# Softmax probabilities: transposes on TensorE replaced by one DMA transpose of fp16 parts per unit

## The chip, the cores and the metric

The kernel runs on one core of a Trainium2 chip. A core has five engines with instruction queues of their own, each worked through in order: TensorE (PE, whose weight loads are listed as PEld), VectorE (DVE), ScalarE (ACT), GpSimd (POOL) and SyncE (SP), whose queue issues all DMAs here. The engines meet through semaphores. The metric is the device time of one execution, in microseconds.

## The reference

Two transformer layers on 1024 tokens of width 1024, in fp32, each with two kinds of attention side by side. Layer one has A (each query keeps the 256 best keys by a cheap indexer's score) and B (a window of 128 with a learned sink); layer two has C (each query attends three times: to compressed blocks, to selected blocks, to a window of 512) and D (latent attention with a rope part). Each has 8 heads. The part that matters, from D:

```python
p = jnp.exp(s - m)
p = p / jnp.maximum(jnp.sum(p, axis=-1, keepdims=True), 1e-30)
o = jnp.einsum('bhqs,bshd->bqhd', p.astype(v.dtype), v)
```

With sequences this short nothing is dropped from C's selection. Scores are large, so products must be near fp32 accuracy.

## The kernel before

Each fp32 operand of a product is held as a high and a low part, and a product is made of three matmuls (high by high, high by low, low by high).

The work is written as Python generators. `attn_gen` yields attention work; `fill_gen` and others yield projection or output matmuls, which `Lanes.run` puts between attention steps by a ratio. A scheduling pass then fixes each engine's final order.

Attention is done by query block of 128 rows (i = 0 to 7) and by group of 4 heads. The unit of work is one pass of the loop over `h0`: as many heads as fit into 1024 columns of scores (4 heads up to 256 keys, 2 up to 512, else 1). So a block with 1, 2, 3, 4 or more times 128 keys is 1, 1, 2, 2 or 4 units. Over a group of 8 blocks A has 22 units, D has 22, B has 8; C has 52, its three branches being 8, 22 and 22. The two groups double this: 208 units. C works through its blocks in the order 0, 1, 4, 5, 6, 7, 2, 3 in group 0 and 0, 1, 2, 3, 6, 7, 4, 5 in group 1.

In a unit TensorE makes the scores (`psS`, line 636), VectorE adds the mask and takes the maximum (`pt`, `nm`, line 639), ScalarE applies Exp (line 644). In groups of up to four 128×128 blocks, `tstage` then transposes the fp32 probabilities on TensorE into PSUM (`psT`, line 664), and they are cut there into fp16 parts `ph` and `pl` in one of two ways, chosen by `WAYS`: "p" has ScalarE write `ph` (668) and VectorE `pl` (669); "q" has ScalarE copy to `sg` (673) and GpSimd make both (674, 675). `cstage` multiplies them with the values into `po` (682 to 684). A unit's transposes are issued about one unit after its scores. C's three branches are added up in `cacc` and stored by a DMA (1295). Weights come by DMA into `wraw` (442), a ring of two, are rounded by ScalarE (446), and GpSimd makes the low part (447).

Of the kernel before, what the change touches and what calls it, by code (L numbers as in the profile page):

```python
# [36 lines left out]
WW = 280  # L37
RG = 0.375
PSCALE = 4096.0
SLOT = 2048  # L40
QB = 3
TR = 1.4
# [12 lines left out]
SR = 0.6  # L55
GDA = [2, 3, 4, 7], [5, 6]
WR = 2
WBF = 14
BO = [2, 3, 0, 1, 4, 5, 6, 7], [2, 3, 0, 1, 4, 5, 6, 7]
AO = list(range(NT)), list(range(NT))  # L60
CO = [0, 1, 4, 5, 6, 7, 2, 3], [0, 1, 2, 3, 6, 7, 4, 5]
# [3 lines left out]
SQB = 1  # L65
RPB = 1
PTC = 1
PHB = 4
PTB = 3
CSB = 1  # L70
SG = 2
WAYS = ('q', 'q', 'ppq', 'pq', 'ppq', 'pq', 'ppq', 'p')
ENG = 'nz zc ky'
ENG2 = 'nz dy ky dq'
MANUAL = False
# [87 lines left out]
def trunk(ctx: ExitStack, tc: tile.TileContext, A, out):  # L163
# [11 lines left out]
    wpool = es_w.enter_context(tc.tile_pool(name="wp", bufs=1, side="right"))  # L175
    dr = ctx.enter_context(tc.tile_pool(name="dr", bufs=1, space=bass.MemoryType.DRAM))
    psA = {n: ctx.enter_context(tc.tile_pool(name=n, bufs=2, space=PSUM)) for n in ("pp", "psS")}
    psT = ctx.enter_context(tc.tile_pool(name="psT", bufs=3, space=PSUM))
    psO = ctx.enter_context(tc.tile_pool(name="psO", bufs=1, space=PSUM))
    if MANUAL:  # L180
        ctx.enter_context(tc.manual_schedule())

# [146 lines left out]
    def tps():  # L329
        return psT.tile([P, 4, P], F32, name="psT")  # L330
# [202 lines left out]
    def v_scale(m, res):  # L533

        yield from L.take_in("psT", PTC)
        ps = tps()
        T.transpose(ps[0:1, 0], m, identf)
        yield
        r = st.tile([P, 2], F32, name="vs_r")
        V.tensor_reduce(r[0:1, 0:1], ps[0:1, 0], AX.X, OP.max)  # L540
        V.tensor_scalar(r[0:1, 0:1], r[0:1, 0:1], 2.0 ** -90, None, op0=OP.max)
        yield
        T.matmul(ps[:, 1, 0:1], r[0:1, 0:1].to_broadcast([1, P]), identf[0:1, 0:1], start=True, stop=True)
        yield
# [6 lines left out]
        V.tensor_scalar(e[:, 0:1], e[:, 0:1], 2.0 ** -15 / PSCALE, None, op0=OP.mult)  # L551
        yield
        res.append((e[:, 1:2], e[:, 0:1]))

# [32 lines left out]

    def attn_gen(jobs):

        tq, cq = [], []  # L590

        def do_T():
            cq.append(tq.pop(0)()[0])

        def do_C():
            cq.pop(0)()

        for jb in jobs:
            while jb.get("drain") and (tq or cq):
                if tq:  # L600
                    do_T()
                else:
                    do_C()
                yield 300
            for ev in jb["need"]:
                yield ev
            nk, npass = jb["nk"], jb["npass"]
# [13 lines left out]
            for h0 in range(0, 4, per):  # L621
# [3 lines left out]
                for j, h in enumerate(hs):  # L625
                    first = init(h)
                    step = 320 if nk == 640 else 512
                    for c in range(0, nk, step):
# [11 lines left out]
                                               -1.0, first, op0=OP.add, op1=OP.min, accum_out=low)  # L640
                        first = low
                        at += w
                for j, h in enumerate(hs):
                    S.activation(pt[:, j * nk:(j + 1) * nk], pt[:, j * nk:(j + 1) * nk], AF.Exp, scale=-1.0,  # L644
                                 bias=nm[:, h:h + 1], accum_out=sm[:, h:h + 1])
                yield per * npass * max(107, nk * 0.42)
                if h0 + per == 4:
# [4 lines left out]
                todo = [(h, kt, j * nk + kt * P) for j, h in enumerate(hs) for kt in range(max(1, nk // P))]  # L652
                if cmp_:
                    todo = [(2 * a, 0, a * P) for a in range(2)]
                for c in range(0, len(todo), 4):
                    grp = todo[c:c + 4]
                    lastg = h0 + per == 4 and c + 4 >= len(todo)

                    def tstage(jb=jb, grp=grp, pt=pt, lastg=lastg, vh=vh, vl=vl, nk=nk, get_po=get_po, fin=fin, cmp_=cmp_,
                               fb=fbox if h0 + per == 4 else None):  # L660
                        n = len(grp)
# [3 lines left out]
                        ph = wk.tile([P, 4, P], F16, name="ph", bufs=PHB)  # L665
                        pl = wk.tile([P, 4, P], F16, name="pl", bufs=PHB)
                        if next(jb["way"]) == "p":
                            S.activation(ph[:, :n], pT[:, :n], AF.Copy, scale=PSCALE)  # L668
                            V.scalar_tensor_tensor(pl[:, :n], pT[:, :n], PSCALE, ph[:, :n], op0=OP.mult,  # L669
                                                   op1=OP.subtract)  # L670
                        else:
                            sg = wk.tile([P, 4, P], F32, name="sg", bufs=SG)
                            S.activation(sg[:, :n], pT[:, :n], AF.Copy, scale=PSCALE)  # L673
                            G.tensor_scalar(ph[:, :n], sg[:, :n], 1.0, 1.0, op0=OP.mult, op1=OP.mult)  # L674
                            G.tensor_tensor(pl[:, :n], sg[:, :n], ph[:, :n], OP.subtract)  # L675

                        def cstage():
                            po = get_po()
                            nt = max(1, nk // P)
                            for a, (h, kt, o) in enumerate(grp):  # L680
                                dst = po[:, h:h + 2].rearrange("p h d -> p (h d)") if cmp_ else po[:, h]
                                T.matmul(dst, ph[:, a], vh(kt, h), start=kt == 0, stop=False)  # L682
                                T.matmul(dst, ph[:, a], vl(kt, h), start=False, stop=False)  # L683
                                T.matmul(dst, pl[:, a], vh(kt, h), start=False, stop=kt == nt - 1)  # L684
                            if lastg:
                                assert fb
                                fin(po, fb[0])
                            return n * 87 + (0 if not lastg else 1)
                        return cstage, n * 110
                    tq.append(tstage)  # L690

                while len(tq) > jb["tlag"](len(todo)):
                    c_, cost = tq.pop(0)()
                    cq.append(c_)
                    yield cost
                    while len(cq) > 1:
                        yield cq.pop(0)()
        while tq:
            c_, cost = tq.pop(0)()
            cq.append(c_)  # L700
            yield cost
            while len(cq) > 1:
                yield cq.pop(0)()
        while cq:
            yield cq.pop(0)()

    def softmax_norm(mul=None):

# [964 lines left out]
    def out_tile(i):  # L1673
        mh = D["mh", i]
        for c in range(2):
            xr = D["pool"].tile([P, 512], F32, name="xr", bufs=XB)
# [121 lines left out]
```

## Time and profile before

| | |
|---|---|
| three runs, median (lowest, highest) | 1559.89 us (1559.67, 1560.49) |
| the profiled execution, its span | 1559.19 us, 1557.4 us |
| busy: TensorE, VectorE, ScalarE, GpSimd | 1384.3, 1226.1, 869.8, 821.4 us |
| mean granted TensorE clock | 0.946 |

The span runs from the first to the last instruction of the profiled execution. Busy time is the union of an engine's instruction times. Matmuls are pipelined and their ends are modelled, so that one instruction's duration is more than the time by which it delays the next; the distance between two starts in the timeline gives that. The parts follow each other so: projections and indexer scores up to about 150 us; the top-k search, with B's units put in between, up to 467; A's two groups up to 628; the first output projection and the second layer's projections up to 840; C, with further projections, up to 1230; D, with the last output projection, to the end.

### The profile page before, as it was taken

How to read it: one execution, taken by the hardware profiler on the slowest of the kernel's cores; microseconds unless marked ns; L12 is line 12 of the kernel's file. 1: busy time of each engine (PE TensorE's matmuls, PEld its weight loads, DVE VectorE, ACT ScalarE, POOL GpSimd, SP SyncE). 2: the span in 40 equal slices, each digit the busy share in tenths (PEclk: the TensorE clock that was granted, in tenths of full speed). 3: DMA queues.
4: the chain of work that ended last, by engine and by line, in shares of the span. 5: the costliest groups of instructions: out<-in, count | busy, mean ns of one | idle time of the engine just before them, and what ended most of it. 6: DMA issues, size and time to landing. Idle time of an engine off the chain costs nothing.

```text
span 1557.4 us, 35155 instructions
## 1 busy us (share of the span) xinstructions
PE 1384.3 (89%) x12588; PEld 1273.9 (82%) x12588; DVE 1226.1 (79%) x3827; ACT 869.8 (56%) x2385; POOL 821.4 (53%) x1097
## 2 busy tenths in 40 slices
PE   6998888788637889999999999999999778889999
PEld 6888878788636779999999998899988556778887
DVE  8599999999998876428338668976689999996763
ACT  6354576577406766325424666956667666754531
POOL 4767642467777657324447343565456565652240
PEclk9999999989867999999999999999999879989999
DMA  6311212111102132332312210012100210111232
GB/s 199 86 35 32 57 56 71 43 36 33 45 17 69 59 107 76 111 108 86 82 36 55 66 49 8 9 47 63 33 15 19 78 62 15 32 55 59 95 112 75
DMA packets 88431, 93.19 MB, mean 60 GB/s; under 512 B 20928, under 2 KB 73152, under 8 KB 88256
## 3 DMA queue, kind: packets, MB, share of 16 engines
q1 hardware_dynamic: 88256, 90.95, 19.3%
q8 instruction: 99, 1.62, 0.4%
q14 instruction: 76, 0.62, 0.1%
HBM read 67.85 MB, written 23.07 MB: 58 GB/s over the span
## 4 chain that ended last, share of the span: by engine, by line
PE 48%; DVE 33%; DMA 6%; POOL 5%; issue 5%; ACT 3%; SPq 0%; POOLq 0%; DVEq 0%; ACTq 0%
PE psS L636 8%; PE pp L490 7%; PE pp L492 6%; PE pp L491 6%; PE psT L664 6%; DVE junk L845 6%; DVE pt L639 4%; PE pp L1683 2%; PE pp L1681 2%; PE pp L1682 2%; PE po L684 2%; PE po L682 2%; PE po L683 2%; DMA wraw<-in_ab_w_in 1%; POOL wlo L447 1%
## 5 line engine op out<-in xcount | busy, mean ns | idle before, releaser
L490 PE MATMUL pp<-whi,Rh 128*128 128x256 f32 (+4 forms) x1648 | 489.1, 297 | 25.9 <-DVE zst L581 9.9
L492 PE MATMUL pp<-whi,Rl 128*128 128x256 f32 (+4 forms) x1648 | 481.0, 292 | 0.6 <-DVE Rl L327 0.6
L491 PE MATMUL pp<-wlo,Rh 128*128 128x256 f32 (+4 forms) x1648 | 480.0, 292 | 0.0
L490 PEld LDWEIGHTS pp<-whi,Rh 128*128 128x128 f32 x1648 | 322.5, 196 | 33.1 <-DVE zst L581 13.9
L644 ACT ACTIVATE pt<-pt,nm 128x256 f32<-128x256 f32 (+8 forms) x384 | 246.6, 643 | 178.6 <-DVE nm L639 173.3
L492 PEld LDWEIGHTS pp<-whi,Rl 128*128 128x128 f32 x1648 | 321.1, 195 | 2.2 <-DVE Rl L327 1.1
L491 PEld LDWEIGHTS pp<-wlo,Rh 128*128 128x128 f32 x1648 | 322.0, 196 | 1.0
L447 POOL TENSOR_TENSOR wlo<-wraw,whi 128x256 fp32r<-128x256 f32 (+4 forms) x208 | 162.3, 787 | 189.6 <-ACT whi L446 176.9
L664 PE MATMUL psT<-identf,pt 128*128 128x128 f32 x1256 | 216.1, 284 | 14.2 <-DVE pl L669 4.2
L674 POOL TENSOR_SCALAR ph<-sg 128x512 f16<-128x512 f32 (+3 forms) x157 | 89.3, 570 | 157.9 <-ACT sg L673 142.0
L664 PEld LDWEIGHTS psT<-identf,pt 128*128 128x128 f32 x1256 | 147.3, 143 | 28.1 <-issue 4.3
L675 POOL TENSOR_TENSOR pl<-sg,ph 128x512 f16<-128x512 f32 (+3 forms) x157 | 163.4, 1041 | 8.7
L446 ACT ACTIVATE whi<-wraw 128x256 fp32r<-128x256 f32 (+4 forms) x208 | 83.7, 416 | 125.0 <-DMA wraw<-in_cd_w_in 37.8
L669 DVE SCALAR_TENSOR_TENSOR pl<-psT,ph 128x512 f16<-128x512 f32 (+3 forms) x233 | 128.4, 556 | 26.8 <-ACT ph L668 26.4
L668 ACT ACTIVATE ph<-psT 128x512 f16<-128x512 f32 (+3 forms) x233 | 111.9, 492 | 51.7 <-PE psT L664 49.2
L684 PEld LDWEIGHTS <-pl 128*128 128x128 f16 x1256 | 114.2, 99 | 26.1 <-issue 7.4
L682 PEld LDWEIGHTS <-ph 128*128 128x128 f16 x1256 | 116.7, 100 | 20.0 <-issue 7.9
L683 PEld LDWEIGHTS <-ph 128*128 128x128 f16 x1256 | 116.7, 100 | 14.7 <-issue 13.5
L639 DVE CUSTOM_DVE_ANT_0 pt<-psS,mk 128x512 f32<-128x512 f32 (+4 forms) x208 | 107.1, 518 | 23.7 <-PE psS L636 21.8
L673 ACT ACTIVATE sg<-psT 128x512 f32<-128x512 f32 (+3 forms) x157 | 83.4, 534 | 32.7 <-PE psT L664 30.1
L344 POOL TENSOR_TENSOR nz<-nz,rs_y 128x512 f32<-128x512 f32 (+2 forms) x44 | 41.2, 937 | 94.0 <-DVE rs_y L288 68.2
L636 PE MATMUL psS<-ka,qs 128*128 128x512 f32 (+4 forms) x192 | 58.7, 405 | 24.1 <-DVE nm L639 23.8
(311 smaller groups left out, 3622.4 us busy)
## 6 DMA issues: line engine op xcount, KB each, us to landing
wraw<-in_cd_w_in SPq DMA_DIRECT2D x72, 128.0 KB, 2.1
wraw<-in_ab_w_in SPq DMA_DIRECT2D x56, 128.0 KB, 2.2
xs<-in_x SPq DMA_DIRECT2D x8, 512.0 KB, 6.0
od<-mx SPq DMA_DIRECT2D x32, 128.0 KB, 1.8
wraw<-in_ab_w_out SPq DMA_DIRECT2D x32, 128.0 KB, 2.2
x<-in_x SPq DMA_DIRECT2D x8, 512.0 KB, 4.6
mo<-od SPq DMA_DIRECT2D x16, 256.0 KB, 2.7
nz<-zdr SPq DMA_DIRECT2D x16, 256.0 KB, 2.8
```

The costliest lines, as they stand in the source:

```text
L447: G.tensor_tensor(lo[:, :o], raw[:, :o], hi[:, :o].bitcast(F32), OP.subtract)
L490: T.matmul(ps, xh, hi[:, :n], start=q == 0 and k == 0, stop=False)
L491: T.matmul(ps, xh, lo[:, :n], start=False, stop=False)
L492: T.matmul(ps, xl, hi[:, :n], start=False, stop=q == 3 and k == 1)
L636: T.matmul(ps[:, at + a - c:at + b - c], lhs, rhs(a, b), start=n == 0, stop=n == len(pl_) - 1)
L639: V.tensor_tensor_reduce(pt[:, j * nk + c:j * nk + c + w], ps[:, at:at + w], mask(c, w), -1.0, first, op0=OP.add, op1=OP.min, accum_out=low)
L644: S.activation(pt[:, j * nk:(j + 1) * nk], pt[:, j * nk:(j + 1) * nk], AF.Exp, scale=-1.0, bias=nm[:, h:h + 1], accum_out=sm[:, h:h + 1])
L664: T.transpose(pT[:, a], pt[:, o:o + P], identf)
L675: G.tensor_tensor(pl[:, :n], sg[:, :n], ph[:, :n], OP.subtract)
L682: T.matmul(dst, ph[:, a], vh(kt, h), start=kt == 0, stop=False)
L683: T.matmul(dst, ph[:, a], vl(kt, h), start=False, stop=False)
L684: T.matmul(dst, pl[:, a], vh(kt, h), start=False, stop=kt == nt - 1)
```

## The change

Probabilities stay in SBUF. ScalarE first adds ln 4096 to the negated maximum `nm`, so that Exp gives them already scaled. It then copies the whole unit to fp16 (`hl`, first half). VectorE or GpSimd, by `WAYS` (all units of B by GpSimd, of the others every second), writes the remainder to the second half. One DMA on SP's queue transposes all blocks of both halves into `ht`. The matmuls with the values read `ht`, one unit later (`LAG`). `hl` and `ht` have two buffers each. The remaining transposes on TensorE (of queries, keys, mixes) have two `psT` banks where there were three, `po` has two where there was one, the ring of prepared weight tiles has 13 where it had 14, and the residual tile `xr` at the end shares a ring with the last weights.

```diff
+LNP = float(np.log(PSCALE))
+HLB = 2
+HTB = 2
+LAG = 1
-WBF = 14
+WBF = 13
-WAYS = ('q', 'q', 'ppq', 'pq', 'ppq', 'pq', 'ppq', 'p')
+WAYS = ('g', 'g', 'dg', 'dg', 'dg', 'dg', 'dg', 'dg')
-    psT = ctx.enter_context(tc.tile_pool(name="psT", bufs=3, space=PSUM))
-    psO = ctx.enter_context(tc.tile_pool(name="psO", bufs=1, space=PSUM))
+    psT = ctx.enter_context(tc.tile_pool(name="psT", bufs=2, space=PSUM))
+    psO = ctx.enter_context(tc.tile_pool(name="psO", bufs=2, space=PSUM))
...
+                S.activation(nm[:, h0:h0 + per], nm[:, h0:h0 + per], AF.Copy, bias=LNP)
                 for j, h in enumerate(hs):
                     S.activation(pt[:, j * nk:(j + 1) * nk], pt[:, j * nk:(j + 1) * nk], AF.Exp, scale=-1.0,
                                  bias=nm[:, h:h + 1], accum_out=sm[:, h:h + 1])
+                n = per * nk
+                hl = wk.tile([P, 2048], F16, name="hl", bufs=HLB)[:, :2 * n]
+                S.activation(hl[:, :n], pt[:, :n], AF.Copy)
+                e = V if next(jb["way"]) == "d" else G
+                e.tensor_tensor(hl[:, n:], pt[:, :n], hl[:, :n], OP.subtract)
+                nb = n // P
+                ht = wk.tile([P, 16, P], F16, name="ht", bufs=HTB)
+                nc.sync.dma_start(ht[:, :2 * nb], hl.rearrange("p (k n) -> p k n", n=P), transpose=True)
...
-                        pT = tps()
-                        for a, (h, kt, o) in enumerate(grp):
-                            T.transpose(pT[:, a], pt[:, o:o + P], identf)
...
+                    for a, (h, kt) in enumerate(todo):
+                        dst = po[:, h:h + 2].rearrange("p h d -> p (h d)") if cmp_ else po[:, h]
+                        T.matmul(dst, ht[:, a], vh(kt, h), start=kt == 0, stop=False)
+                        T.matmul(dst, ht[:, a], vl(kt, h), start=False, stop=False)
+                        T.matmul(dst, ht[:, nb + a], vh(kt, h), start=False, stop=kt == nt - 1)
...
+                cq.append(cstage)
+                while len(cq) > LAG:
+                    yield from cq.pop(0)()
```

ScalarE's queue, in C at block 7 of group 0 (the four heads of the selected branch, 1024 columns each; `ph` and `sg` are read from PSUM), before:

```order
L644 ACTIVATE pt_14002,sm_14001<-pt_14002,nm_14000 128x1024
L644 ACTIVATE pt_13931,sm_13930<-pt_13931,nm_13929 128x64 x2
L673 ACTIVATE sg_14024<-psT_14019 128x256
L644 ACTIVATE pt_14035,sm_14001<-pt_14035,nm_14000 128x1024
L668 ACTIVATE ph_14057<-psT_14052 128x512
L668 ACTIVATE ph_14097<-psT_14092 128x512
L644 ACTIVATE pt_14121,sm_14001<-pt_14121,nm_14000 128x1024
L673 ACTIVATE sg_14145<-psT_14138 128x512
L668 ACTIVATE ph_14172<-psT_14167 128x512
L644 ACTIVATE pt_14198,sm_14001<-pt_14198,nm_14000 128x1024
```

The same place now, with the changed file's line numbers (638 is Exp, 642 the copy to `hl`, 636 the bias):

```order
L642 ACTIVATE hl_12780<-pt_12768 128x1024
L638 ACTIVATE pt_12813,sm_12767<-pt_12813,nm_12766 128x1024
L636 ACTIVATE nm_12766<-nm_12766 128x1
L642 ACTIVATE hl_12825<-pt_12813 128x1024
L638 ACTIVATE pt_12867,sm_12767<-pt_12867,nm_12766 128x1024
L636 ACTIVATE nm_12766<-nm_12766 128x1
L638 ACTIVATE pt_12925,sm_12767<-pt_12925,nm_12766 128x1024
L642 ACTIVATE hl_12879<-pt_12867 128x1024
L636 ACTIVATE nm_12976<-nm_12976 128x1
L638 ACTIVATE pt_12978,sm_12977<-pt_12978,nm_12976 128x640
L642 ACTIVATE hl_12937<-pt_12925 128x1024
```

The two reads of PSUM per unit are gone; a copy to `hl` stands between the Exps, and from the third unit of the block on it stands one Exp later than its own.

SP's queue at the same place now (1268 is the store of a finished block of C, whose last transpose is that of `ht_12674`). Before, this stretch held only such stores and weight loads:

```order
L647 DMA_TRANSPOSE ht_12592<-hl_12589 128x10x128
L647 DMA_TRANSPOSE ht_12635<-hl_12632 128x10x128
L647 DMA_TRANSPOSE ht_12674<-hl_12671 128x10x128
L647 DMA_TRANSPOSE ht_12725<-hl_12722 128x4x128
L1268 DMA od2_101<-cacc_12360 128x256
L647 DMA_TRANSPOSE ht_12783<-hl_12780 128x16x128
L647 DMA_TRANSPOSE ht_12828<-hl_12825 128x16x128
L647 DMA_TRANSPOSE ht_12882<-hl_12879 128x16x128
L647 DMA_TRANSPOSE ht_12940<-hl_12937 128x16x128
```

One transpose per unit has come in, of 4 to 16 blocks, and the store stands between the transposes of the following block.

## Rows read from the trace of the kernel before

**Rows 1.** The page: busy time, share of the span and instructions of each engine.

```profile
PE 1384.3 (89%) x12588; PEld 1273.9 (82%) x12588; DVE 1226.1 (79%) x3827; ACT 869.8 (56%) x2385; POOL 821.4 (53%) x1097
```

**Rows 2.** By stretch: start:end, length, busy PE, PEld, DVE, ACT, POOL; clock, DMA.

```profile
150.00:467.00 317.00, 240.25 (x1964) 229.26 (x1963) 310.60 (x861) 176.32 (x482) 183.23 (x219) 0.89 0.16 45
467.00:546.00 79.00, 66.45 (x677) 54.37 (x678) 67.97 (x189) 53.83 (x131) 55.27 (x65) 0.85 0.21 67
546.00:628.00 82.00, 75.11 (x871) 67.62 (x870) 55.79 (x169) 55.22 (x130) 55.13 (x67) 0.98 0.31 91
628.00:840.00 212.00, 211.27 (x1757) 208.51 (x1754) 108.35 (x319) 79.65 (x217) 85.12 (x124) 0.98 0.26 78
840.00:941.00 101.00, 100.36 (x1049) 97.75 (x1048) 69.33 (x271) 61.82 (x189) 47.33 (x67) 1.00 0.21 58
941.00:1010.00 69.00, 67.39 (x830) 58.16 (x829) 60.70 (x227) 56.66 (x162) 31.99 (x44) 1.00 0.03 10
1010.00:1134.00 124.00, 123.80 (x1265) 120.74 (x1264) 86.45 (x315) 74.89 (x227) 68.06 (x89) 1.00 0.16 46
1134.00:1230.00 96.00, 84.38 (x968) 75.79 (x967) 88.47 (x397) 65.08 (x211) 56.15 (x89) 0.98 0.10 31
1230.00:1400.00 170.00, 135.94 (x1146) 113.78 (x1147) 160.88 (x508) 112.05 (x296) 103.40 (x132) 0.86 0.14 45
1400.00:1557.00 157.00, 153.80 (x1177) 128.42 (x1175) 97.04 (x270) 61.74 (x152) 39.94 (x52) 1.00 0.26 85
```

**Rows 3.** Line 664, transposes of probabilities, by stretch: length, PE, PEld; clock, DMA.

```profile
546.00:628.00 82.00, 22.65 (x138) 15.64 (x136) 0.98 0.31 91
...
840.00:941.00 101.00, 20.17 (x111) 13.33 (x111) 1.00 0.21 58
...
1010.00:1134.00 124.00, 22.95 (x130) 15.22 (x130) 1.00 0.16 46
...
1400.00:1557.00 157.00, 20.76 (x130) 14.83 (x128) 1.00 0.26 85
```

**Rows 4.** The timeline of PE in C: start, duration, instruction.

```profile
970.50 1.09 PE L664 MATMUL psT<-identf,pt 128*128 128x128 f32 x8
971.35 1.17 PE L636 MATMUL psS<-ks,qs 128*128 128x512 f32 x4
```

**Rows 5.** Groups, partly by shape: busy us, mean ns; idle us before, releasers.

```profile
L668 ACT ACTIVATE ph<-psT 128x512 f16<-128x512 f32 (+3 forms) x233 | 111.9, 492 | 51.7 <-PE psT L664 49.2 <-PE po L683 1.0 <-PE po L684 0.8
L673 ACT ACTIVATE sg<-psT 128x512 f32<-128x512 f32 (+3 forms) x157 | 83.4, 534 | 32.7 <-PE psT L664 30.1 <-POOL pl L675 1.2 <-PE psS L636 0.4
L669 DVE SCALAR_TENSOR_TENSOR pl<-psT,ph 128x512 f16<-128x512 f32 x133 | 90.5, 682 | 12.1 <-ACT ph L668 11.7
L675 POOL TENSOR_TENSOR pl<-sg,ph 128x512 f16<-128x512 f32 x121 | 142.1, 1175 | 6.5
L510 ACT ACTIVATE pt<-x 128x1024 f32<-128x1024 f32 x8 | 8.5, 1059 | 1.7 <-DVE x L1091 1.7
L1588 ACT ACTIVATE sq<-pp 128x128 f32<-128x128 f32 x16 | 4.7, 294 | 0.0
```

**Rows 6.** Line 669, VectorE's low parts, by stretch: length, DVE; clock, DMA.

```profile
467.00:546.00 79.00, 15.03 (x27) 0.85 0.21 67
...
1230.00:1400.00 170.00, 20.37 (x34) 0.86 0.14 45
```

**Rows 7.** DMA issues: count, KB each, median us to landing.

```profile
x1d<-x SPq DMA_DIRECT2D x8, 512.0 KB, 3.0
...
wraw<-in_ab_w_in SPq DMA_DIRECT2D x8, 16.0 KB, 1.7
...
pe<-in_c_cmp_pe SPq DMA_DIRECT2D x2, 8.0 KB, 4.7
```

**Rows 8.** Waits of SP's queue: us in total, times, longest.

```profile
SPq L442 <- POOL wlo L447: 363.3, 160, 27.8
SPq L1295 <- POOL cacc L1293: 147.6, 16, 22.5
```

More of the change, by code (lines that the diff above doesn't have):

```diff
@@ L67 @@
 PTC = 1
-PHB = 4
 PTB = 3
 CSB = 1
-SG = 2
-WAYS = ('q', 'q', 'ppq', 'pq', 'ppq', 'pq', 'ppq', 'p')
+WAYS = ('g', 'g', 'dg', 'dg', 'dg', 'dg', 'dg', 'dg')
 ENG = 'nz zc ky'
@@ L550, in v_scale @@
         V.tensor_scalar(e[:, 1:2], e[:, 1:2], 2.0 ** 14, None, op0=OP.mult)
-        V.tensor_scalar(e[:, 0:1], e[:, 0:1], 2.0 ** -15 / PSCALE, None, op0=OP.mult)
+        V.tensor_scalar(e[:, 0:1], e[:, 0:1], 2.0 ** -15, None, op0=OP.mult)
         yield
@@ L588, in attn_gen @@
     def attn_gen(jobs):
[L590 to L596, printed above, removed]
-        for jb in jobs:
[L599 to L604, printed above, removed]
+        cq = []
+        for jb in jobs:
+            while jb.get("drain") and cq:
+                yield from cq.pop(0)()
             for ev in jb["need"]:
@@ L645, in attn_gen @@
                                  bias=nm[:, h:h + 1], accum_out=sm[:, h:h + 1])
+                n = per * nk
[6 more added lines that the diff above has]
+                nc.sync.dma_start(ht[:, :2 * nb], hl.rearrange("p (k n) -> p k n", n=P), transpose=True)
                 yield per * npass * max(107, nk * 0.42)
-                if h0 + per == 4:
+                last = h0 + per == 4
+                if last:
                     if jb.get("free"):
@@ L651, in attn_gen @@
                     L.post(jb["norm"](nm, sm, fbox))
-                todo = [(h, kt, j * nk + kt * P) for j, h in enumerate(hs) for kt in range(max(1, nk // P))]
+                todo = [(h, kt) for h in hs for kt in range(max(1, nk // P))]
                 if cmp_:
[L654 to L661, printed above, removed]
-                        pT = tps()
-                        for a, (h, kt, o) in enumerate(grp):
-                            T.transpose(pT[:, a], pt[:, o:o + P], identf)
[L665 to L703, printed above, removed]
+                    todo = [(0, 0), (2, 0)]
+                def cstage(todo=todo, ht=ht, nb=nb, last=last, vh=vh, vl=vl, nk=nk, get_po=get_po, fin=fin, cmp_=cmp_,
+                           fb=fbox if last else None):
+                    po = get_po()
+                    nt = max(1, nk // P)
+                    for a, (h, kt) in enumerate(todo):
[3 more added lines that the diff above has]
+                        T.matmul(dst, ht[:, nb + a], vh(kt, h), start=False, stop=kt == nt - 1)
+                        if a % 4 == 3 and a + 1 < len(todo):
+                            yield 4 * 87
+                    if last:
+                        assert fb
+                        fin(po, fb[0])
+                    yield (len(todo) - 1) % 4 * 87 + 88
@@ L704, in attn_gen @@
+                cq.append(cstage)
+                while len(cq) > LAG:
+                    yield from cq.pop(0)()
         while cq:
-            yield cq.pop(0)()
+            yield from cq.pop(0)()
     def softmax_norm(mul=None):
@@ L1675, in out_tile @@
         for c in range(2):
-            xr = D["pool"].tile([P, 512], F32, name="xr", bufs=XB)
+            xr = D["pool"].tile([P, 512], F32, name="xr", tag="wraw2", bufs=WB)
             cs_ = slice(512 * c, 512 * c + 512)
```

## The prediction

> **What bounds the kernel now.** I read the engines' totals first [rows 1]: TensorE counts as busy for 89% of the span, VectorE for 79%, ScalarE for 56%, GpSimd for 53%. That average hides the limits, so the next view is busy time by stretch [rows 2], cut where one attention group's Exps begin or end. The reader is to see three kinds of stretch. In 150–467 (top-k search with the sliding-window units, called B here) VectorE has 310.6 of 317 us and TensorE 240: VectorE sets the end. In 628–840, 840–941, 1010–1134 and 1400–1557 TensorE has all but 0.2 to 3.2 us: attention there runs beside projection or output matmuls and TensorE sets the end. In the dense stretches, where attention is nearly alone, no engine is full: 467–546 (PE 66, DVE 68 of 79), 546–628 (75 and 56 of 82), 941–1010 (67 and 61 of 69), 1134–1230 (84 and 88 of 96). A unit here goes from engine to engine, and its time is that of a loop over few buffers. Counting units from the code (see the section on the kernel), these four stretches hold 22, 22, 28 and 31 units, so one takes 3.6, 3.7, 2.5 and 3.1 us. In 1230–1400 (start of D, the last attention) VectorE has 161 of 170 us.
>
> So a microsecond of TensorE is worth a microsecond only in the second kind of stretch; in the dense ones what counts is how soon a unit's probabilities come back transposed.
>
> **What is removed from TensorE.** 1256 transposes. One occupies TensorE not for the 0.28 us of its row but for the distance to the next start: eight begin at 970.50 and what follows begins at 971.35, 0.106 us each [rows 4]. All of them are 133 us. The stretches where TensorE sets the end hold 111, 130 and 130 [rows 3]: 12, 14 and 14 us, together −40. Those in B lie under VectorE's work and are worth nothing.
>
> **What moves on ScalarE, VectorE and GpSimd.** Before, ScalarE read each group of up to four blocks from PSUM, 111.9 + 83.4 = 195 us in all [rows 5]; then VectorE took 0.68 us for a full group, or GpSimd two passes, the second of 1.18 us. Now ScalarE copies the whole unit from SBUF (nearest row, L510, 1.06 us for 1024 columns) and adjusts the bias (nearest small row, L1588, 0.29 us, an upper end; the lower is nothing). The columns are those of 157 full units, 166 us, and 208 bias copies are 60 us at most: up to 31 us more than before. In the tightest stretch, 941–1010, that is 20.5 × 1.06 + 28 × 0.29 = 30 us for 24, and ScalarE has 12 us free there, so I take nothing; without that room it would be the 6 us. The subtraction covers 1024 columns at once; its SBUF source is not in the trace, so I price it by the rows of 512 columns doubled, 1.36 us on VectorE and 2.35 on GpSimd, 1.86 in the mean of the alternating units; the ends are half of VectorE's row, 0.68, and GpSimd's 2.35. In D the share of VectorE falls: 20.4 us of such work in 1230–1400 [rows 6] become 9 full units by 1.36, 12.2: −8 us, in a stretch that VectorE sets.
>
> **What is added: 208 DMA transposes.** No row shows one. A full unit is 512 KB from SBUF to SBUF, that is 2048 rows of 128 elements, each to be laid over 128 partitions. From below: a plain 512 KB store lands in 3.0 us [rows 7]. From above: if each of a full unit's 16 blocks had to land before the next, 16 small DMAs by the row of 16 KB at 1.7 us, 27 us. Nearest in kind is the one rearranging load, 2048 scattered elements, 4.7 us. I count both jobs, bytes 3.0 and pieces 4.7: **7.7 us for a full unit**, of which 1.7 (the smallest row) don't shrink with size: 1.7 + 6.0k for a unit of k times 1024 columns.
>
> Now the loop. There are two hl buffers, so ScalarE's copy for unit u+2 waits for the transpose of u; the rows of the order on ScalarE show that copy queued ahead of later Exps, which then wait as well, and after them VectorE's maxima and TensorE's scores. Two units thus fit into one pass of copy, subtraction and transpose: per unit (1.06k + 1.86k + 1.7 + 6.0k)/2 = 0.85 + 4.46k us. With mean k of 0.82, 0.82, 0.73 and 0.65:
> 467–546: 22 × 4.50 = 99 against 79, +20.
> 546–628: 99 against 82, +17.
> 941–1010: 28 × 4.11 = 115 against 69, +46.
> 1134–1230: 31 × 3.76 = 117 against 96, +21.
> Elsewhere the loop hides: in 840–941 24 units of k 0.60 need 85 of 101 us, in 1010–1134 21 of 0.70 need 84 of 124, B needs 16 × 5.0 = 80 of 317, D 44 × 4.5 = 198 of 327. If that cover is gone, as when the queue runs late, each costs what the loop exceeds it by.
>
> **SP's queue.** Each transpose stands in line with weight loads and stores. SP waits 147.6 us for the accumulators of C's stores, up to 22.5 at once, and 363.3 us for weight buffers that GpSimd frees [rows 8]. Today that costs nothing, since nothing urgent stands behind; now a transpose may. The order on SP puts the store of a finished block one unit behind its last transpose, and the transpose behind that store needs the same unit's matmuls done anyway, for its ht buffer; so of a price between 0 and those 147.6 us I take 0, and let the other end widen the range. 208 issues at a third of a microsecond are part of the landing.
>
> **Small edits.** One weight buffer fewer, one transpose bank fewer (its remaining users take turns through one permit), the output's residual tile sharing a ring with the last weights, the scale moved into the Exp's bias, a second bank for outputs: hidden by prefetch and by TensorE's queue; without that cover the residual load costs its landing, some 3 us for each of 16. I take 0.
>
> **The sum.** +20 + 17 + 46 + 21 − 40 − 8 = +56 us on the profiled execution's 1559.2 us (span 1557.4), which is 0.7 below the runs' median: about **1615 us**. Only the landing time is soft: each microsecond of its variable part moves the sum by 38 us (half of the 77 full units in the dense stretches), so the change breaks even at 7.7 − 56/38 = 6.2 us for a full unit.
>
> A table of the Trainium skill (VectorE: DVE Perf Modes, "The three transpose paths") speaks against the change: 390 ns for a 128×128 block on TensorE, 1309 ns by DMA. The rows differ for the first, 0.106 us between starts. Taken one by one, the 2512 blocks (high and low parts) at 1309 ns would be, as an estimate, 754, 1466 and 754 us of transposing in A, C and D against the 161, 390 and 327 that these take now; by that the sum would be near 3.7 ms.
>
> **Rivals.**
> (1) *The landing is that of a plain store*, 3.0 us. The loop falls to 0.85 + 2.1k, 57 us for 22 units in A and 67 for the 28: other limits take over, VectorE in 467–546 (68 − 15.0 of its subtractions + 12.2, so 65: −14), TensorE's freed time in 546–628 (−15), −2 in 941–1010 (the loop's 67 of 69), −7 in 1134–1230 (VectorE's 88 of 96, hardly changed); with −48 from elsewhere −86: **1473 us**. It decides as soon as a full unit lands in under 6.2 us. For it: the 512 KB store, and queues that the trace shows 3 to 31% busy in the dense stretches [rows 2]. Against: the store moves no element to another partition. The Trainium skill has a rule for this side (Advanced Engine Details and Errata, "X-Bar Transpose (TRN2)"): transposes as fast as regular DMAs. No run here shows it yet.
> (2) *Transposes run strictly one after another* and their stream is the bound, at the same 7.7. A and C can't hold it: 44 × 6.6 = 290 against 161, +129; C's 104 units × 5.7 = 597 against 390, +207; the freed time in late D and VectorE's −8 remain, −22: **1873 us**. For it: one queue issues them all, in order. Against: the trace has several DMAs in flight on it.
> (3) *Block by block*, 27 us for a full unit: 36, 70 and 36 full units in A, C and D, +3100: **4660 us**. Against: one instruction covers a whole unit.
> (4) *The change does nothing measurable*: landing between 6.1 and 6.3, or gains and stalls cancel: **1559 us**.
>
> **How the numbers follow.** A measurement here tells 0.2%, about 3 us, from no change. The forecast, from 6.3 to about 11 us for a full unit, gets 0.38, and its own range is 1565 to 1750. Rival 1, with all landings below 6.1, 0.37, because its row is a plain 512 KB move on the same queue. Rival 4 gets 0.05, rival 2 0.15, rival 3 0.05. Faster 0.37, same 0.05, slower 0.58. For 8 in 10 I leave out rival 3, the quickest tenth of rival 1 and rival 2's slower third: **1485 to 1900 us**, both signs inside.
>
> **What would show it.** Right: the transpose issues land in 6 to 9 us for 512 KB; ScalarE's hl copies and TensorE's first matmul on ht wait for a DMA; the 28 units of C's group 0 (blocks 6, 7, 2, 3) take above 100 us; 628–840 keeps its length; the projection stretches of C lose about 12 us each. Wrong: landings of 3 to 5 us with TensorE full in C; or SP seen issuing one transpose for microseconds, with loads and stores waiting behind; or a chain led by SP's stores.

## The result and the profile after

The changed kernel takes 1666.42 us (median of four runs, 1663.92 to 1668.69) against 1560.19 us for the kernel before beside it (four runs, 1559.67 to 1564.15): a ratio of 1.0675, 95% interval 1.0651 to 1.0698. It is slower, as forecast, inside the range, and by nearly twice the forecast +56. The reasons given for it hold only in part.

The first row to set against [rows 1] is that of the totals: busy time, share of the span and instructions of each engine in the changed kernel, whose span is 1666.9 us.

```profile
PE 1336.6 (80%) x11332; PEld 1206.5 (72%) x11332; DVE 1216.5 (73%) x3690; ACT 893.3 (54%) x2411; POOL 783.5 (47%) x895
```

TensorE has 1256 instructions and 48 us less, in a span that is 110 us longer. The next rows are the stretches of [rows 2], cut at the same work: start:end, length, busy PE, PEld, DVE, ACT, POOL, then the granted clock, the share of the DMA engines and GB/s.

```profile
0.00:153.00 153.00, 127.21 (x940) 121.15 (x941) 124.88 (x321) 79.04 (x207) 100.78 (x158) 0.98 0.30 90
153.00:491.00 338.00, 231.04 (x1878) 217.88 (x1876) 325.51 (x890) 177.93 (x490) 192.25 (x206) 0.85 0.30 71
491.00:580.00 89.00, 62.79 (x519) 47.26 (x520) 50.62 (x149) 54.73 (x122) 26.95 (x17) 0.63 0.73 148
580.00:667.00 87.00, 62.31 (x677) 52.07 (x674) 54.23 (x146) 54.82 (x128) 38.78 (x36) 0.87 0.85 172
667.00:904.00 237.00, 227.15 (x1840) 223.87 (x1841) 115.12 (x351) 83.13 (x227) 94.60 (x134) 0.95 0.29 78
904.00:1011.00 107.00, 97.22 (x979) 93.68 (x978) 68.57 (x264) 64.83 (x203) 41.66 (x46) 0.95 0.61 120
1011.00:1101.00 90.00, 66.43 (x597) 51.10 (x598) 56.77 (x198) 61.55 (x165) 28.55 (x23) 0.68 0.67 124
1101.00:1230.00 129.00, 122.55 (x1259) 118.94 (x1258) 95.79 (x400) 76.63 (x267) 56.98 (x71) 0.99 0.50 104
1230.00:1340.00 110.00, 77.60 (x663) 63.13 (x663) 83.31 (x302) 71.96 (x187) 57.27 (x53) 0.63 0.67 138
1340.00:1513.00 173.00, 120.25 (x956) 99.20 (x954) 152.03 (x442) 105.96 (x274) 86.36 (x95) 0.77 0.45 95
1513.00:1667.00 154.00, 142.07 (x1042) 118.21 (x1041) 89.69 (x238) 62.73 (x150) 59.32 (x60) 0.97 0.62 142
```

Three things are to be seen. In the dense stretches (491–667, 1011–1101, 1230–1340) no engine is near full, and the DMA engines, 3 to 31% busy before, now have 67 to 85%. TensorE idles there, and its granted clock, a mean over the levels 1.2 and 2.4 GHz, falls from 0.85, 0.98, 1.00 and 0.98 to 0.63, 0.87, 0.68 and 0.63. And time was also lost where nothing was forecast: 338 us for 317 in B, 237 for 212 in the projections after A.

Who waits for the transposes, in the whole kernel (us in total, times, longest), and then the view of the tile `ht`: the issue with its duration on SP's queue (ns, smallest, median, largest) and the landing:

```profile
PEld L665 <- DMA ht<-hl: 112.4, 93, 4.2
ACT hl L642 <- DMA ht<-hl: 87.2, 68, 4.8
PE po L665 <- DMA ht<-hl: 85.3, 67, 3.9
```

```profile
L647 SPq DMA_TRANSPOSE ht<-hl x208: 1188/1518/5880, 184.6 to 1647.3; - x104
DMA to landing us min/median/max: 2.4/4.1/9.4
```

Taken apart by size, the 16 smallest units (4 blocks in the two halves) land in 2.46 us in the median, the 62 full ones (16 blocks) in 4.44: 0.165 us per block behind a fixed 1.8, so T = 1.8 + 2.64k where the prediction had 1.7 + 6.0k.

The ring itself, from the timeline in C (start, duration, instruction, idle time and its end):

```profile
1021.28 7.77 SPq L647 DMA_TRANSPOSE ht<-hl  x3
1021.75 0.95 ACT L642 ACTIVATE hl<-pt 128x896 f16<-128x896 f32 x1 [1.05 <-DMA ht<-hl]
1022.83 1.90 POOL L644 TENSOR_TENSOR hl<-pt,hl 128x896 f16<-128x896 f32 x1 [3.73 <-ACT nm L636]
1025.62 0.95 ACT L642 ACTIVATE hl<-pt 128x896 f16<-128x896 f32 x1 [1.87 <-DMA ht<-hl]
1025.64 0.24 PE L665 MATMUL po<-vhs,ht 128*128 128x64 f16 x1 [1.34 <-DMA ht<-hl]
1026.60 1.09 DVE L644 TENSOR_TENSOR hl<-pt,hl 128x896 f16<-128x896 f32 x1 [0.64 <-ACT hl L642]
1028.71 0.74 ACT L642 ACTIVATE hl<-pt 128x640 f16<-128x640 f32 x1 [1.04 <-DMA ht<-hl]
```

A copy into `hl` begins the moment an earlier transpose lands (1021.75, 1025.62, 1028.71); its subtraction follows, then its transpose (the first row merges three issues), and with two buffers its landing frees the copy two units on. TensorE's matmuls start on the same landing.

### The profile page after: what moved, and what is told of

Read it like the earlier page. It is cut to its first block, busy times and chain, and to the rows that moved or that the text cites. A ratio compares the mean times of both kernels' runs of the same rounds, so it can differ in the third digit from the quotient of the medians.

```text
span 1666.9 us, 32673 instructions
## 1 busy us (share of the span) xinstructions
PE 1336.6 (80%) x11332; PEld 1206.5 (72%) x11332; DVE 1216.5 (73%) x3690; ACT 893.3 (54%) x2411; POOL 783.5 (47%) x895
## 3 DMA queue, kind: packets, MB, share of 16 engines
q1 hardware_dynamic: 416448, 173.29, 46.9%
## 5 line engine op out<-in xcount | busy, mean ns | idle before, releaser
L494 PEld LDWEIGHTS pp<-whi,Rl 128*128 128x128 f32 x1648 | 326.3, 198 | 5.8 <-DVE Rl L329 4.6
L644 POOL TENSOR_TENSOR hl<-pt,hl 128x1024 f16<-128x1024 f32 (+5 forms) x112 | 189.8, 1694 | 292.3 <-ACT hl L642 229.3
L642 ACT ACTIVATE hl<-pt 128x1024 f16<-128x1024 f32 (+5 forms) x208 | 175.2, 844 | 90.3 <-DMA ht<-hl 87.2
L665 PEld LDWEIGHTS <-ht 128*128 128x128 f16 x1256 | 128.8, 109 | 124.8 <-DMA ht<-hl 112.4
L666 PEld LDWEIGHTS <-ht 128*128 128x128 f16 x1256 | 130.9, 110 | 0.4 <-issue 0.2
L667 PEld LDWEIGHTS <-ht 128*128 128x128 f16 x1256 | 130.8, 110 | 0.1
L644 DVE TENSOR_TENSOR hl<-pt,hl 128x640 f16<-128x640 f32 (+5 forms) x96 | 103.0, 1073 | 33.4 <-ACT hl L642 33.2
L636 ACT ACTIVATE nm<-nm 128x1 f32<-128x1 f32 (+2 forms) x208 | 41.1, 199 | 160.2 <-DVE nm L632 159.7
L629 PE MATMUL psS<-ka,qs 128*128 128x512 f32 (+4 forms) x192 | 67.3, 465 | 63.0 <-DVE nm L632 62.3
L629 PEld LDWEIGHTS psS<-ka,qs 128*128 128x128 f32 x192 | 39.8, 252 | 74.5 <-DVE nm L632 72.4
L629 PE MATMUL psS<-kw,qs 128*128 128x320 f32 (+4 forms) x192 | 58.2, 407 | 23.3 <-DVE nm L632 23.3
L638 ACT ACTIVATION_READ_ACCUMULATOR pt<-pt,nm 128x1 f32 x384 | 72.5, 189 | 0.0
```

Source lines behind the costliest of these rows:

```text
L494: T.matmul(ps, xl, hi[:, :n], start=False, stop=q == 3 and k == 1)
L629: T.matmul(ps[:, at + a - c:at + b - c], lhs, rhs(a, b), start=n == 0, stop=n == len(pl_) - 1)
L642: S.activation(hl[:, :n], pt[:, :n], AF.Copy)
L644: e.tensor_tensor(hl[:, n:], pt[:, :n], hl[:, :n], OP.subtract)
L665: T.matmul(dst, ht[:, a], vh(kt, h), start=kt == 0, stop=False)
L666: T.matmul(dst, ht[:, a], vl(kt, h), start=False, stop=False)
```

## The experiments

Lengths in us of the stretches of nine kernels, cut where the Exps of the units named begin (the dense ones begin and end with their own Exps; the gaps behind them count with what follows). "C, 24 units" is group 0's blocks 0, 1, 4, 5, "C, 28" its blocks 6, 7, 2, 3, "C, 21" and "C, 31" those of group 1.

| | before | after | no trip | plain copy | small edits | two DMAs | cuts | third hl | idle transposes |
|---|---|---|---|---|---|---|---|---|---|
| up to A | 468 | 492 | 490 | 485 | 458 | 490 | 485 | 484 | 484 |
| A, group 0 (dense) | 78 | 88 | 64 | 81 | 88 | 76 | 97 | 92 | 86 |
| A, group 1 (dense) | 82 | 87 | 73 | 76 | 92 | 71 | 89 | 83 | 89 |
| projections | 213 | 238 | 230 | 235 | 221 | 264 | 250 | 247 | 242 |
| C, 24 units | 101 | 107 | 98 | 97 | 108 | 104 | 100 | 99 | 110 |
| C, 28 (dense) | 69 | 89 | 68 | 83 | 71 | 84 | 89 | 85 | 86 |
| C, 21 | 124 | 130 | 122 | 130 | 129 | 132 | 128 | 122 | 142 |
| C, 31 (dense) | 96 | 110 | 101 | 103 | 105 | 99 | 120 | 107 | 97 |
| gap and D, group 0 | 159 | 160 | 153 | 154 | 164 | 164 | 169 | 166 | 200 |
| D, group 1, end | 168 | 167 | 154 | 159 | 179 | 161 | 163 | 159 | 181 |
| span | 1557 | 1667 | 1552 | 1603 | 1615 | 1646 | 1690 | 1644 | 1716 |

**No trip.** The matmuls read `hl` itself.

```diff
-                ht = wk.tile([P, 16, P], F16, name="ht", bufs=HTB)
-                nc.sync.dma_start(ht[:, :2 * nb], hl.rearrange("p (k n) -> p k n", n=P), transpose=True)
+                ht = hl.rearrange("p (k n) -> p k n", n=P)
```

> The changed kernel without the DMA: the matmuls read the untransposed parts hl, so products with the values are of the wrong elements; all other work and its order stay. Theory L (the unit's loop through the landing of 4.4 us for a full unit, with the idle TensorE and its lower clock behind it): the dense stretches fall back below those of before and the total comes to 1470 to 1500 us. Theory O (part of the +106 comes from the new order of the work, the +20 at the end of B and the +25 in the projections after A, and has nothing to do with the trip): 1510 to 1560. If the copies and subtractions on ScalarE, VectorE and GpSimd are the cost: above 1600.

Measured: 1551.62 us, ratio to the kernel before 0.9941 (0.9919 to 0.9962). Against the changed kernel's 1.0675 the trip through the DMA costs 0.0734 of 1560, 115 us. The other half of the reading is as important: with the trip left out the change brings 9 us, not the 48 of the forecast gains, and the 22 us up to A and the 17 in the projections are still lost. That is the range of theory O, with theory L half right on the dense stretches: the 64 and 73 us lie below before, the 68 equals it, the 101 of the last lies above. The run leaves one wait in that a free trip need not have: without `ht` the matmuls hold `hl` itself a unit longer, and ScalarE waits for them (us in total, times, longest):

```profile
ACT hl L642 <- PE po L666: 23.4, 19, 6.0
```

So the 9 us are what this run gained, not a strict limit.

**A plain copy of the same bytes.**

```diff
-                nc.sync.dma_start(ht[:, :2 * nb], hl.rearrange("p (k n) -> p k n", n=P), transpose=True)
+                nc.sync.dma_start(ht[:, :2 * nb], hl.rearrange("p (k n) -> p k n", n=P))
```

> The changed kernel with a plain DMA of the same bytes from hl to ht in place of the transposing one (blocks arrive untransposed, so the products are of the wrong elements). If the transposing is what is dear, a full unit lands in about 3 us, the DMA engines are far less busy, and the total is 1490 to 1540 us. If any trip through a DMA costs it: 1600 or more, with landings near 4 us.

Measured: 1608.05 us, 1.0296 (1.0272 to 1.0320). The queue's totals (packets, MB, share of 16 engines) and the landing of the full units (KB each, median us) with the copy, then the totals in the changed kernel:

```profile
q1 hardware_dynamic: 118208, 173.28, 31.7%
...
ht<-hl SPq DMA_DIRECT2D x62, 512.0 KB, 3.1
```

```profile
q1 hardware_dynamic: 416448, 173.29, 46.9%
```

So of the 115 us about half, 0.0355 of 1560 or 55 us, is any trip that lands in 3.1 us, and 59 is the transposing: 1.3 us more on a full unit's landing, the same 173 MB in 3.5 times the packets. The issue on SP, which the landing time includes, is longer by about as much (2.0 us for 0.47 on a full unit); whether the one makes the other is not shown. Both expectations failed in part: 1490 to 1540, for the transposing alone being dear, in the time; 1600 or more, for any trip, in its landings, which are at 3.1 and not near 4.

**The small edits alone**, on the kernel before, and then **the banks alone**.

```diff
-WBF = 14
+WBF = 13
...
-    psT = ctx.enter_context(tc.tile_pool(name="psT", bufs=3, space=PSUM))
-    psO = ctx.enter_context(tc.tile_pool(name="psO", bufs=1, space=PSUM))
+    psT = ctx.enter_context(tc.tile_pool(name="psT", bufs=2, space=PSUM))
+    psO = ctx.enter_context(tc.tile_pool(name="psO", bufs=2, space=PSUM))
...
-            xr = D["pool"].tile([P, 512], F32, name="xr", bufs=XB)
+            xr = D["pool"].tile([P, 512], F32, name="xr", tag="wraw2", bufs=WB)
```

> The kernel before with the small edits alone (13 weight buffers, two transpose banks, two banks for outputs, the residual tile in the ring of the last weights). My step, which took these at nothing: 1556 to 1563 us. The rival, that the +20 at the end of B or the +25 in the projections comes from them: 1580 to 1605.

> The kernel before with two banks for transposes (three before) and two for outputs (one before), nothing else. The small edits together cost 58 us of 1560. If it is the missing bank for TensorE's 1256 transposes of probabilities, this one shows all of it: 1610 to 1625. If it is the weight ring or the residual tile's ring: 1556 to 1565.

Measured: 1617.66 us, 1.0365 (1.0340 to 1.0390) for all four edits, above both ranges, and 1609.19 us, 1.0308 (1.0285 to 1.0330) for the two lines on banks. In the kernel before, then, edits that I took at nothing cost 57 us, of which the banks are 48. They don't lengthen what stands ahead of A (458 us for 468), so the +24 there is not theirs. Where the third bank is missing shows in the reads of `psT` by ScalarE with the banks alone (busy us, mean ns, idle before, its releasers), against 51.7 of idle time in [rows 5]:

```profile
L668 ACT ACTIVATE ph<-psT 128x512 f16<-128x512 f32 (+3 forms) x233 | 112.4, 492 | 89.2 <-PE psT L664 82.0 <-PE psS L636 2.5 <-PE po L683 1.3
```

But these are waits for transposes of probabilities, which the changed kernel doesn't make. So the banks were given back to that one:

```diff
-    psT = ctx.enter_context(tc.tile_pool(name="psT", bufs=2, space=PSUM))
-    psO = ctx.enter_context(tc.tile_pool(name="psO", bufs=2, space=PSUM))
+    psT = ctx.enter_context(tc.tile_pool(name="psT", bufs=3, space=PSUM))
+    psO = ctx.enter_context(tc.tile_pool(name="psO", bufs=1, space=PSUM))
```

> The changed kernel with three banks for transposes and one for outputs, as before. If the bank cost only as long as probabilities were transposed on TensorE, the changed kernel does not need it: 1655 to 1690 (one bank for outputs may cost a little). If the missing bank is still felt in the changed kernel: 1600 to 1640.

Measured: 1659.00 us, 1.0635 (1.0606 to 1.0665), 6 us better than the changed kernel, with intervals that overlap. There the banks cost little or nothing; the step held in the changed kernel, for a reason it did not give.

**Two DMAs per unit**, each half in its own buffers.

```diff
...
+                S.activation(hh, pt[:, :n], AF.Copy)
+                nc.sync.dma_start(hht[:, :nb], hh.rearrange("p (k n) -> p k n", n=P), transpose=True)
...
+                e.tensor_tensor(ll, pt[:, :n], hh, OP.subtract)
+                nc.sync.dma_start(llt[:, :nb], ll.rearrange("p (k n) -> p k n", n=P), transpose=True)
...
```

> The high and the low half in buffers of their own, each with a transpose of its own; the high half leaves as soon as ScalarE has written it. Same bytes, twice as many DMAs. Theory L: 8 blocks land in 3.1 us, the longer loop (low half) falls from 3.4 to about 2.4 us for a full unit, the total to 1600 to 1640. If the 16 DMA engines or SP's issues (2 x 1.24 us for 2.0 us) are the bound: 1665 to 1720.

Measured: 1652.69 us, 1.0580 (1.0554 to 1.0605): faster than the changed kernel by 0.0095, 15 us, less than expected. The landings are at 3.0 us in the median of all sizes (3.3 for 8 blocks, where 3.1 was expected), and the four dense stretches shrink from 373 to 330 us in sum; but the projections take 264 for 238. What the units saved, TensorE did not use for other work beside them: A holds 20 projection products for 48, the projections 511 for 486.

**More fill.** Each attention step reports again the 110 ns a block that its transposes had reported.

```diff
-                yield per * npass * max(107, nk * 0.42)
+                yield per * npass * max(107, nk * 0.42) + nb * 110
```

> The changed kernel with 110 ns for each block of probabilities added again to what an attention step reports, as the transposes on TensorE did, so that projection matmuls are put beside attention by the same account as before. Theory O (the +25 in the projections after A are matmuls that moved there out of the attention stretches, where TensorE idles at a lower clock): projections shorter by 10 to 25, total 1635 to 1655, clock up. If the dense stretches are held by the loop of the units alone and hold no such room: 1660 to 1680.

Measured: 1662.07 us, 1.0639 (1.0610 to 1.0668): not told apart from the changed kernel. The rows on the first of the three matmuls of a projection product, in A and then in the projections, count the products (x; then busy us, mean ns, idle before): before the change, then after it, then in this run.

```profile
L490 PE MATMUL pp<-whi,Rh 128*128 128x256 f32 x64 | 18.7, 294 | 0.0
...
L490 PE MATMUL pp<-whi,Rh 128*128 128x256 f32 (+1 forms) x463 | 133.9, 290 | 0.7 <-DVE x L1091 0.6
```

```profile
L492 PE MATMUL pp<-whi,Rh 128*128 128x256 f32 x48 | 16.4, 342 | 1.0 <-ACT Rh L328 1.0
...
L492 PE MATMUL pp<-whi,Rh 128*128 128x256 f32 (+1 forms) x486 | 141.4, 293 | 1.1 <-DVE sm L691 0.8 <-ACT Rh L328 0.3
```

```profile
L492 PE MATMUL pp<-whi,Rh 128*128 128x256 f32 x48 | 14.4, 301 | 1.9 <-ACT Rh L328 1.9
...
L492 PE MATMUL pp<-whi,Rh 128*128 128x256 f32 (+1 forms) x484 | 141.6, 294 | 4.7 <-DVE sm L691 2.9 <-DVE zst L583 1.3 <-ACT gat L1246 0.3
```

A holds 16 products less and the projections hold 23 more, but the one does not feed the other. Those 16 stand ahead of A now (688 for 672 up to A's start). The 23 come from C, behind the projections (426 for 450 over its four stretches), and nearly all of them from its last, dense one, before the change and after it:

```profile
L490 PE MATMUL pp<-whi,Rh 128*128 128x160 f32 x61 | 17.2, 282 | 0.0
```

```profile
L492 PE MATMUL pp<-whi,Rh 128*128 128x160 f32 x4 | 1.1, 266 | 0.0
```

The reported cost is not what moved them, since with it given back A still holds 48 and the projections 484.

**Matmuls on ht two units later.**

```diff
-LAG = 1
+LAG = 2
```

> The changed kernel with the matmuls on ht two units after the scores instead of one. If TensorE, which stands in line at the first matmul on ht while scores of later units are behind it, is what costs (198 us of waits on the landing): 1600 to 1645. If the ring of two hl and two ht sets the pace, TensorE only waits elsewhere and ht comes free later: 1660 to 1700.

Measured: 1656.55 us, 1.0613 (1.0591 to 1.0634), 10 us better, between the two ranges. TensorE's place in line is not what holds the units: ScalarE's wait for the landing is 83.2 us here for 87.2, and the dense stretches take 371 us in sum for 373.

**A third hl, and its control.**

```diff
-HLB = 2
+HLB = 3
...
-WBF = 13
+WBF = 11
...
-YD = 3
-NZ = 4
+YD = 2
+NZ = 3
```

> The changed kernel with three hl instead of two; to make room 11 weight buffers instead of 13, NZ 3 instead of 4, YD 2 instead of 3 (the next run has these cuts alone). Theory L: from the copy into hl to the landing a unit takes 7.4, 8.3, 6.5 and 6.4 us in the dense stretches and two buffers give the measured pace of 3.6, 4.1, 3.3 and 3.6; with three the next limit is the two ht (landing, matmuls, issue, about 5.8 / 2 = 2.9), so the dense stretches shorten by 0.4 to 1.2 us for each of 103 units, 40 to 75 us against the next run. If the DMA engines (share 0.66 to 0.85 there) or TensorE's line at ht set the pace: less than 10 us against the next run.

> The changed kernel with 11 weight buffers, NZ 3 and YD 2, and still two hl: the control of the run above. Between 1665 and 1700 us; what it exceeds 1666 by is the price of these rings.

Measured: 1651.03 us, 1.0598 (1.0549 to 1.0647) with the third buffer, 1689.23 us, 1.0825 (1.0786 to 1.0865) with the cuts alone. The third buffer is worth 0.0227, 35 us, just short of the 40 to 75 expected, and more than the 23 us that the cuts cost. ScalarE's wait for the landing, first with the cuts, then with three buffers:

```profile
ACT hl L642 <- DMA ht<-hl: 71.8, 67, 5.7
```

```profile
ACT hl L642 <- DMA ht<-hl: 32.1, 23, 4.1
```

From the start of each copy to its landing, and from one unit's Exp to the next, means over a stretch's units worked out from the trace (us; the first divided by the number of buffers stands beside it):

| | after | cuts | third hl |
|---|---|---|---|
| A, group 0 | 7.36 / 2 = 3.68; pace 3.64 | 7.64 / 2 = 3.82; 4.25 | 9.94 / 3 = 3.31; 3.94 |
| A, group 1 | 8.32 / 2 = 4.16; 4.07 | 8.57 / 2 = 4.28; 4.18 | 10.44 / 3 = 3.48; 3.91 |
| C, 28 units | 6.46 / 2 = 3.23; 3.25 | 6.44 / 2 = 3.22; 3.24 | 7.51 / 3 = 2.50; 3.10 |
| C, 31 units | 6.43 / 2 = 3.22; 3.62 | 6.89 / 2 = 3.45; 3.99 | 7.28 / 3 = 2.43; 3.53 |

In the changed kernel the first three paces are those of the ring to 3%. With three buffers the ring is no longer it, and the pace gains only 0.1 to 0.5. The dense stretches shorten by 28 us in sum against the cuts alone, where leaving the trip out of the changed kernel shortens them by 67: the two buffers are less than half of what the trip costs there. The limit named for what comes next, 2.9 us by two `ht`, is not reached (3.1 to 3.9), and what takes over was not traced to one wait.

**Transposes on TensorE that nobody reads**, put ahead of the matmuls on `ht`.

```diff
...
+                    for c in range(0, nb, 4):
+                        pT = tps()
+                        for j in range(c, min(c + 4, nb)):
+                            T.transpose(pT[:, j - c], pt[:, j * P:j * P + P], identf)
```

> The changed kernel with the 1256 fp32 transposes of probabilities put back on TensorE ahead of the matmuls on ht, into psT, with nobody reading them: TensorE's time is as before, the DMA trip stays. If TensorE's lower clock in the dense stretches (0.63 to 0.87 against 0.85 to 1.00 before), which comes from its idling, is what makes them long: clock above 0.9 there and a total of 1620 to 1655. Theory L (the pace is that of the hl ring, with TensorE outside it): the clock rises, the pace stays at 3.3 to 4.1 us for a unit, and the stretches where TensorE is nearly full lose up to 12 to 14 us each: 1665 to 1710.

Measured: 1720.23 us, 1.1024 (1.0986 to 1.1063), above both ranges. The dense stretches, in the order of the rows above:

```profile
484.00:570.00 86.00, 67.11 (x665) 55.54 (x664) 60.79 (x160) 56.27 (x132) 41.86 (x37) 0.88 0.76 147
570.00:658.00 88.00, 71.57 (x815) 60.56 (x816) 52.41 (x141) 54.64 (x123) 37.69 (x33) 0.94 0.86 172
1011.00:1097.00 86.00, 65.35 (x691) 51.62 (x691) 53.24 (x173) 56.79 (x149) 25.64 (x20) 0.92 0.62 114
1239.00:1336.00 97.00, 75.41 (x789) 63.15 (x786) 58.15 (x204) 56.73 (x141) 26.52 (x25) 0.86 0.60 109
```

The clock is back at 0.86 to 0.94 and three of the four are as long as they were, within 4 us: there the lower clock came with the waiting and is not what makes them long, unless the transposes' own time hides a gain. In the last, where the pace had been above the ring's, it went from 110 to 97; the clock is a candidate for those 12 us, not shown alone. The kernel as a whole is 54 us slower than the changed one, but not in the length of the stretches where TensorE was said to set the end: the 24 units of C take 110 for 107, the 21 without the gap ahead of them 96 for 100, D's second group up to its last Exp 145 for 145. Most is in the gaps: 46 us for 29 ahead of the 21 units, 70 for 36 ahead of D, 35 for 22 behind the last Exp. Part of it is TensorE's work all the same, put off from beside attention into the gaps; here are the projection products of the first gap and of the second:

```profile
L492 PE MATMUL pp<-whi,Rh 128*128 128x256 f32 x96 | 28.4, 297 | 1.1 <-ACT nz L1332 1.1
...
L492 PE MATMUL pp<-whi,Rh 128*128 128x160 f32 x24 | 6.9, 286 | 0.0
```

In the changed kernel the first gap has 67 and the second none. How much of the gaps this explains stays open; two banks carry 1256 more transposes here as well.

**Transposes issued by ScalarE.**

```diff
-                nc.sync.dma_start(ht[:, :2 * nb], hl.rearrange("p (k n) -> p k n", n=P), transpose=True)
+                nc.scalar.dma_start(ht[:, :2 * nb], hl.rearrange("p (k n) -> p k n", n=P), transpose=True)
```

> The changed kernel with the transposes issued by ScalarE instead of SP. If the one queue is what costs outside the loop (loads and stores behind transposes that wait for data, transposes behind loads): the projections after A get shorter by 10 to 20 us and landings in A fall from 4.4 to 4.8 towards 4.0; total 1630 to 1660. ScalarE pays with the time of the issue, 1.2 to 2.0 us of 208 as seen on SP; if that stands in the unit's loop, the dense stretches lengthen by 0.6 to 1 us a unit and the total is 1700 to 1800.

Measured: 1729.51 us, 1.1087 (1.1046 to 1.1128).

```profile
L647 ACTq DMA_TRANSPOSE ht<-hl x208: 1205/1448/6293, 187.8 to 1705.1; - x104
DMA to landing us min/median/max: 2.4/4.2/11.5
```

The issue takes as long as on SP, now out of ScalarE's time in the ring; the dense stretches grow to 93, 97, 102 and 121 us, by 0.2 to 0.5 us a unit where 0.6 to 1 was expected. The projections stay at 240, so it was not SP's queue that lengthened them, and the landing's median is no shorter; in A it is 4.7 and 5.3 us in the mean, where 4.0 was expected.

## Why the prediction came out as it did

The direction was right and the total inside the range, but that is luck, by terms that cancel: the ring cost 55 us less than forecast, the gains of 48 turned into a loss of 11, and 49 came where nothing was forecast. In the profiled executions, 110 us longer in span, and by the table's first two columns to a tenth:

1. **The landing, 7.7 us for a full unit: wrong.** It is 4.44. The fixed part was right (1.8 for 1.7), the part that grows with size less than half (2.64 for 6.0); counting 4.7 us of pieces on top of the bytes was the fault. The bytes were priced right, 3.0 for the 3.1 of the plain copy, and the rearranging adds 1.3 to that. The rule cited with rival 1 (the Trainium skill, Advanced Engine Details and Errata, "X-Bar Transpose (TRN2)": as fast as regular DMAs) doesn't hold here either: 4.44 against 3.1 us for the same 512 KB. Nor does the price of one 128×128 block by DMA (the Trainium skill, VectorE: DVE Perf Modes, "The three transpose paths": 1309 ns, in a table for bf16) carry over to many blocks in one DMA: here a further block adds 165 ns.

2. **The loop of two hl: right as a mechanism, its price too low for the landing measured.** Copy, subtraction, transpose and landing divided by two give the pace in three of the four dense stretches, and a third buffer takes 35 us off. But the prediction's terms with the measured landing, (1.06k + 1.86k + 1.8 + 2.64k)/2, make 3.2 us in A and 2.9 and 2.7 in C, where 3.6, 4.1, 3.3 and 3.6 were measured. With the shorter landing its price is +10, +4, +21 and +14, together +49, not +104.

3. **TensorE's freed time, −40, and VectorE's −8: failed.** This is the step that broke the break-even. In place of −12, −14, −14 and −8 the four stretches changed by +6, +5, −1 and +1. Without the trip they changed by −3, −3, −14 and −6, so even then about half came: all of it in D's second group, little in C. The 24 units of C show where it went without the trip (start:end, length, busy as in the rows above):

```profile
856.00:954.00 98.00, 97.04 (x1012) 93.44 (x1010) 68.95 (x265) 65.99 (x203) 41.67 (x46) 0.99 0.19 55
```

TensorE is still full. By the distances from one start to the next, worked out from the trace, its transposes are gone there, 9.9 us, but it makes 174 projection products for 160, 3.9 us more, and its matmuls on scores and values take 2.6 us more. The products came forward from C's last stretch, where TensorE had room (84 of 96 us) and their going shortened nothing (101 for 96). The sentence "elsewhere the loop hides" failed too: with the trip TensorE waits for `ht` in those stretches (97.2 busy of 107 us where it had 100.4 of 101), and they are 37 us dearer than without. Given its transposes back, TensorE makes the 24 units 3 us longer and puts products off into the gaps.

4. **Priced at nothing: B and what stands ahead of it, +24, the projections, +25.** The run without the trip has +22 and +17, so most of it comes from the order of the work. In B VectorE sets the end and is busy 325.5 us for 310.6. In the projections TensorE's product matmuls take 13 us more (9 without the trip, with 481 products), with the products that came forward from C. I had read the order on ScalarE and SP, not TensorE's. What moved the products is open; it is neither the reported cost nor SP's queue.

5. **SP's queue at nothing, small edits at nothing:** an issue was counted at a third of a microsecond and takes 1.52 in the median, 363 us of SP for the 208. SP's share was tried only by moving the transposes to ScalarE, where the price of the issue covers whatever SP's queue may have cost inside the ring; outside it nothing came back. The banks are worth some 6 us in the changed kernel, not clear of noise, but 48 in the kernel before, where the same step would have been wrong by all of it.

The break-even of 6.2 us is refuted by the copy: at 3.1 us for a full unit the kernel is 46 us slower than before, and rival 1, with a landing of 3.0, gave 1473. Of the signs named ahead, the waits of ScalarE and TensorE for a DMA came; the others speak against it: a full unit lands in 4.44 us and not in 6 to 9, the 28 units take 89 us and not above 100, the 212 us of 628–840 became 237, and SP issues one transpose for up to 5.88 us. Rival 2 falls on landings that overlap (two full units landed 2.4 us apart, taking 4.4 and 4.8 from issue to landing, where it has 7.7 for each in line), rival 3 on 4.44 for 27, rival 4 on the ratio. Rival 3's +3100 doesn't come out of its terms: 142 full units by 27 us, less the 878 us that A, C and D take, are 2960. By item 1 alone, with the rest of my sum kept, I should have forecast a gain of some 70 us (56 less 3.4 times 38); from there to the loss of 110 it is some 73 us by item 2's price, 59 by item 3 and 49 by item 4.

No run here is faster than the kernel before but the one without the trip, and that by 0.6%, 9 us. The cheapest trip that a run shows, the plain copy, costs 55.

## What to carry to other kernels

Price a trip through memory by the ring it stands in, (copy + subtraction + landing) / buffers, and take that as a lower end (the paces here were 0.3 to 0.9 us above it); but first ask what leaving the whole trip out would bring: one such run gave 9 us, and would have told most of it. TensorE at 99% of a stretch does not mean that its removed work comes back as time: D's second group gave all of it back, C's stretches little, since the order of the work filled the room with products from a stretch that had room for them. Count an engine's work by stretch before and after, and not its share alone. And a bank or a buffer taken "for nothing" has to be priced in the kernel that still uses it: the same banks were worth 48 us in one and some 6, not clear of noise, in the other.

## What the runs showed of the hardware

- A DMA that transposes fp16 blocks from SBUF to SBUF lands in 1.8 us + 0.165 us per 128×128 block (2.46 for 4, 4.44 for 16), against 2.0 and 3.1 us for plain copies of the same bytes.
- It is not free for the queue that issues it: 1.19 to 5.88 us for one issue, median 1.52 (2.0 for 16 blocks), on SP, and about the same on ScalarE (1.21 to 6.29), where a plain copy of the same bytes took 0.47 in the median.
- It keeps the DMA engines busy for longer than a plain copy does: with the loads and stores on the same queue 46.9% of the 16 engines' time over the span, against 31.7% with plain copies, for the same 173 MB. In A's second group all DMA together had 85%.
